# Moving, shortening and joining the branches around the rare token lots of a mixture of experts

## The chip, the cores and the metric

The kernel runs on one core of a Trainium2 chip, as one program. The metric is the device time of one execution in microseconds (us). The engines are named as the profile names them: PE (matrix products, with PEld for the weights that it loads), ACT, DVE, POOL, and SP, which issues the DMAs. A name with a q (PEq, SPq) is the engine's sequencer or its queue of DMAs.

## The reference, cut to what matters

The program is a first block of two dense layers and a second block of two layers. Each layer of the second block ends in a mixture of 32 experts in four groups: a router picks the best group of a token and two experts in it, and every token goes through its two experts. Layer 0 has 512 tokens (256 of `x` and 256 of the context), layer 1 has 256.

```python
def hier_moe(h, grp_w, grp_b, exp_w, exp_b, w_gate, w_up, w_down):
    g_logit = (h @ grp_w).astype(jnp.float32) + grp_b.astype(jnp.float32)
    g_idx = jnp.argmax(g_logit, axis=-1).astype(jnp.int32)
...
    top_v, top_i = lax.top_k(e_logit, TOP_K)
    w = (g_prob * jax.nn.softmax(top_v, axis=-1)).astype(h.dtype)
    e_idx = g_idx[:, None] * EXPERTS_PER_GROUP + top_i.astype(jnp.int32)
    return routed_experts(h, e_idx, w, w_gate, w_up, w_down)

    def expert_block(args):            # in routed_experts
        xblk, e = args
        return (jax.nn.silu(xblk @ w_gate[e]) * (xblk @ w_up[e])) @ w_down[e]
```

`w_gate` and `w_up` of an expert are 1024 x 512, `w_down` is 512 x 1024, all float32. How many tokens an expert gets is known only when the program runs.

## The kernel before, in words

Everything that the change touches is in `experts`, which writes the program of one layer's experts. It is written out without a loop over the experts: the 32 experts stand in the code one after the other, as 16 pairs, once for layer 0 and once for layer 1.

**Slots and lots.** An expert has CAP = 64 slots for tokens, in two lots of LOT = 32. The first lot is always computed. The second is computed inside `If(count > LOT)` (L2070), and whatever goes beyond 64 tokens inside `If(count > CAP)` (L2084, in `more`). Those are the rare lots. Their counts lie in the table `cnt`, and each of the engines that has work in the branch (PE, ACT, DVE, and POOL in layer 0) loads the count into a register (L1870) and jumps on its own. Entries from NE on hold the larger count of each pair; the kernel before uses only the last of these, the largest of all, after the experts (`rest`, L2142).

**A pair, in the order in which PE meets it.** The names S, M and J are this document's:

- `expert(p, 0)`: `gate_up` of the first lot (L2010, 64 products of 32 slots by 256 columns over four weight tiles), branch S0 (L2070), `combine` of half of the previous pair's result (L1986), `turn_lots` (two transposes, L1921), branch M0 (L2084), whose body `more_gate_up` gathers 32 more tokens and does `gate_up` for them.
- `expert(p, 1)`: the same for the second expert: `gate_up`, branch S1, the other half of `combine`, `turn_lots`, `slots` (transposes, L1945), branch M1.
- `down(p)`: `project` for both experts together (L1960, 32 products of 64 slots by 512 columns), which ACT and DVE then weigh (L1953, L1954), after every second pair `gather` for the next two pairs (L1895), and branches J0 and J1 (L2084 both), whose body `more_project` projects what `more_gate_up` left.

So PE meets six branches a pair, 96 a layer. Whether a body runs or not, its instructions stand in the program, and an engine that does not need them jumps over them.

**Weights.** A pair needs twelve tiles of 1 MB: four `gu` for each expert and four `down`. SP issues their DMAs (L315) in the order of use into rings of 1 MB buffers, 14 buffers in layer 0 and 18 in layer 1. A buffer is given to a later tile when the last instruction that could read it has been passed, which for `gu` is in the branches M0 and M1 and for `down` in J0 and J1. `K.addn` names the tiles of a step; a tile is given back after the last step that names it.

Of the kernel before, what the change touches and what calls it, by code (L numbers as in the profile page):

```python
# [11 lines left out]
F32R = mybir.dt.float32r  # L12
# [6 lines left out]
P = 128  # L19
# [1653 lines left out]
class _Moe:  # L1673
# [87 lines left out]
    def experts(self, i, rms=None, side=None, tail=None):  # L1761
# [150 lines left out]
        def lot(hs, i, xk, ws):  # L1912
            gu = K.pt("acc")[:, :256]
            gate_up(gu, xk, ws)
            hidden(hs[:, i * P:i * P + P], gu)

# [39 lines left out]
        def project(hTa, hTb, a0, b0, a1, b1, wsl):  # L1956
            ys = [K.pt("acc"), K.pt("acc")]
            for c, n in ((c, n) for b in (0, 2) for n in range(2) for c in (b, b + 1)):
                for s, (hT, ws) in enumerate(((hTa, (a0, a1)), (hTb, (b0, b1)))):
                    mm(ys[n][64 * s:64 * s + 64], lhsT=hT[:, at(c)], rhs=part(ws, c)[:, n * 512:n * 512 + 512],  # L1960
                       start=c == 0, stop=c == 3, tile_position=(0, 64 * s), skip_group_check=True)
            yh, yl = (B.new(n, [P, D], F32R) for n in ("yh", "yl"))
# [56 lines left out]
        def more_gate_up(Pm, wt, ws, parts):  # L2019
# [19 lines left out]
            turn(hs, hT)  # L2039

        def more_project(parts, ws):
            hT, PT, wsl = parts
            ps = K.pt("acc")[:, :256]
            for c, q in enumerate(quarters):
                by_quarter(ps, hT[:, q], lambda q: part(ws, c)[:, 256 * q:256 * q + 256], start=c == 0, stop=c == 3)
            yh, yl = more_new(F32R), more_new(F32R)
            weigh(yh, yl, ps, wsl)
            for d in range(KC):
                q = quarters[d // 2]
                f = slice(d % 2 * P, d % 2 * P + P)  # L2050
                ps = K.pt()[:, :N]
                kw = dict(rhs=PT[q], tile_position=(LOT * (d // 2), 0))
# [4 lines left out]
        def expert(p, s):  # L2057
            def fn(*ws):
                e = 2 * p + s
                if e == 0:  # L2060
# [3 lines left out]
                xg, hs = B._t[f"xg{p // 2}"], B._t[f"hs{s}"]  # L2064
                o = (p % 2) * 2 * CAP
                if s == 1:
                    pw = weighed(B._t[f"P{p // 2}"][:, :, o:o + 2 * CAP], B.wt[:, :, e - 1:e + 1])
                x = lambda i: lambda k: xg[:, k, o + s * CAP + i * LOT:o + s * CAP + i * LOT + LOT]
                lot(hs, 0, x(0), ws)
                with K.tc.If(count(e, engines[:3]) > LOT):  # L2070
                    lot(hs, 1, x(1), ws)
                if p > 0:
                    combine(s, *B.y)
                turn_lots(hs, B.new(f"hT{s}", [P, 4 * CAP]))
                if s == 1:
                    PT, wsl = B._t["slots"] = B.new("PT", [P, N], F32R), B.new("wsl", [P, 1], bufs=2)
                    slots(pw, PT, wsl)
                parts = B._t[f"more{s}"] = more_parts(s)
                more(e, lambda: more_gate_up(first_lot(e), wt(e), ws, parts))
# [6 lines left out]

        def down(p, turns):
            def fn(*ws):
                PT, wsl = B.slots
                if turns:  # L2090
                    pick((p + 1) // 2)()
                B._t["y"] = (*project(B.hT0, B.hT1, *ws, wsl), PT)
                if turns:
                    gather((p + 1) // 2)()
                for s in range(2):
# [173 lines left out]
```

## Time and profile before

| | us |
|---|---|
| median of 3 runs | 2289.48 (2288.54 to 4694.85) |
| the profiled execution | 2281.83 |
| its span, first to last instruction | 2280.1 |
| of that the experts of layer 0 | 996 to 1556 |
| of that the experts of layer 1 | 1783 to 2262 |

The two stages are read off the timeline: from the first gathered tokens to the last rare projection, and to the branch of `rest`. The profiled execution is a single one, and 7.65 us shorter than the median of the runs. In the rows below, a group of instructions shows its count, and in square brackets the idle time of the engine ahead of its first instruction and what ended it. "<-PEq L2084" means that PE's own sequencer, at a branch of line 2084, was the last thing before PE went on; "<-issue" that the engine waited for nothing that the profile shows.

### The profile page before, as it was taken

The numbers are of one execution on the slowest core, as the hardware profiler recorded it, in microseconds if no ns is written. First come the engines' busy times: TensorE is split into PE (matmuls) and PEld (weight loads), VectorE is DVE, ScalarE is ACT, GpSimd is POOL, SyncE is SP. The second block draws the span as 40 slices with busy tenths as digits, with TensorE's granted clock in tenths as the row PEclk, the third lists the DMA queues.
The fourth block names the chain that finished last, engine by engine and source line by source line (L and its number), as shares of the span: only waits on it lengthen the run. The fifth ranks groups of instructions, "written<-read, shape, count | busy, mean of one in ns | idle before, by whom it ended". The sixth has DMA issues, their size and how long they took to land. (4 is left out here: it accounts for less than half of the span.)

```text
span 2280.1 us, 40150 instructions
## 1 busy us (share of the span) xinstructions
PE 1937.3 (85%) x15978; PEld 1510.0 (66%) x15978; DVE 1059.4 (46%) x1974; ACT 750.7 (33%) x1347; POOL 450.4 (20%) x496
## 2 busy tenths in 40 slices
PE   7889999998799987888888978887999787777776
PEld 6768998987799866655555655554877444444443
DVE  7665774576567579533223432335554312122123
ACT  5554653553456355421111111113453111111111
POOL 4122420999954016100000000001000000000000
PEclk9899999999999999989999899998999889889898
DMA  6477566444355453669997799982224899999993
GB/s 238 175 300 268 213 240 243 165 137 159 111 177 175 168 186 138 239 273 369 380 382 318 303 388 377 380 322 70 95 74 193 335 406 414 413 386 418 408 411 137
DMA packets 86478, 603.51 MB, mean 265 GB/s; under 512 B 9632, under 2 KB 12064, under 8 KB 13856
## 3 DMA queue, kind: packets, MB, share of 16 engines
q1 hardware_dynamic: 86176, 599.24, 67.6%
q8 instruction: 219, 3.59, 0.6%
q14 instruction: 83, 0.68, 0.1%
HBM read 598.15 MB, written 1.05 MB: 263 GB/s over the span
## 5 line engine op out<-in xcount | busy, mean ns | idle before, releaser
L405 PE MATMUL mm<-xh,wh 128*128 128x256 f32 x1024 | 294.8, 288 | 20.4 <-ACT wh L382 16.3
L407 PE MATMUL mm<-xh,wl 128*128 128x256 f32 x1024 | 292.9, 286 | 9.5 <-DVE wl L383 8.5
L406 PE MATMUL mm<-xl,wh 128*128 128x256 f32 x1024 | 292.8, 286 | 0.6 <-DVE xl L480 0.3
L1960 PE MATMUL acc<-down,hT 128*64 128x512 f32 x1024 | 242.2, 619 | 37.6 <-PEq L2084 35.1
L2010 PE MATMUL acc<-gu,xg 128*32 128x256 f32 x2944 | 185.7, 411 | 47.6 <-PEq L2084 28.8
L405 PEld LDWEIGHTS mm<-xh,wh 128*128 128x128 f32 x1024 | 199.1, 194 | 30.9 <-ACT wh L382 17.4
L1910 DVE TENSOR_TENSOR hs<-hs,acc 128x128 f32<-128x128 f32 x81 | 23.3, 287 | 418.6 <-ACT hs L1909 404.6
L1960 PEld LDWEIGHTS acc<-down,hT 128*64 128x64 f32 x1024 | 131.2, 142 | 128.1 <-issue 101.5
L2010 PE MATMUL acc<-gu,xc 128*32 128x256 f32 x2240 | 156.8, 432 | 60.6 <-PEq L2084 49.4
L407 PEld LDWEIGHTS mm<-xh,wl 128*128 128x128 f32 x1024 | 198.7, 194 | 11.1 <-DVE wl L383 9.9
L406 PEld LDWEIGHTS mm<-xl,wh 128*128 128x128 f32 x1024 | 199.1, 194 | 1.8 <-DVE xl L480 1.6
L2010 PEld LDWEIGHTS acc<-gu,xg 128*32 128x32 f32 x2944 | 115.5, 118 | 115.7 <-issue 72.2
L2010 PEld LDWEIGHTS acc<-gu,xc 128*32 128x32 f32 x2240 | 91.1, 124 | 123.5 <-issue 62.5
L1909 ACT ACTIVATE hs<-acc 128x128 f32<-128x128 f32 x81 | 22.4, 277 | 410.1 <-PE acc L2010 404.4
L1954 DVE SCALAR_TENSOR_TENSOR yl<-acc,wsl,yh 128x512 fp32r<-128x512 f32 x64 | 48.0, 751 | 224.9 <-ACT yh L1953 209.6
L383 DVE TENSOR_TENSOR wl<-ffn_w_up,wh 128x1024 fp32r<-128x1024 f32 x96 | 130.3, 1382 | 28.6 <-ACT wh L382 28.6
L405 PE MATMUL mm<-hh,wh 128*128 128x256 f32 (+1 forms) x416 | 128.5, 309 | 7.6 <-DVE cv L1250 5.9
L882 DVE SCALAR_TENSOR_TENSOR hv<-mm,vec,hv 128x255 f32<-128x255 f32 x192 | 88.2, 480 | 85.1 <-ACT hv L877 81.1
L406 PE MATMUL mm<-hl,wh 128*128 128x256 f32 (+1 forms) x416 | 124.3, 299 | 0.7 <-DVE hl L480 0.4
L407 PE MATMUL mm<-hh,wl 128*128 128x256 f32 (+1 forms) x416 | 123.8, 298 | 0.5 <-DVE wl L383 0.3
L1953 ACT ACTIVATE yh<-acc,wsl 128x512 fp32r<-128x512 f32 x64 | 44.0, 687 | 239.5 <-PE acc L1960 239.5
L424 POOL TENSOR_TENSOR xc<-xc,tot 128x256 f32<-128x256 f32 x4 | 2.9, 728 | 596.7 <-ACT tot L421 596.7
(494 smaller groups left out, 4461.4 us busy)
## 6 DMA issues: line engine op xcount, KB each, us to landing
gu<-in_gu_dram SPq DMA_DIRECT2D x256, 1024.0 KB, 10.9
down<-in_down_dram SPq DMA_DIRECT2D x128, 1024.0 KB, 11.3
mod_w<-in_mod_w_dram SPq DMA_DIRECT2D x48, 1024.0 KB, 4.9
ffn_w_up<-in_ffn_w_up_dram SPq DMA_DIRECT2D x48, 1024.0 KB, 4.9
ffn_w_down<-in_ffn_w_down_dram SPq DMA_DIRECT2D x24, 1024.0 KB, 4.8
w_in_ab<-in_w_in_ab_dram SPq DMA_DIRECT2D x12, 1024.0 KB, 4.8
kv_w<-in_kv_w_dram SPq DMA_DIRECT2D x8, 1024.0 KB, 6.7
w_out_ab<-in_w_out_ab_dram SPq DMA_DIRECT2D x8, 1024.0 KB, 4.8
```

What stands on the lines that cost most here:

```text
L383: self.lows.append(lambda: nc.vector.tensor_sub(wl, src, wh))
L405: mm(out, lhsT=wh(k), rhs=xh(k), start=s, stop=False, **kw)
L406: mm(out, lhsT=wh(k), rhs=xl(k), start=False, stop=False, **kw)
L407: mm(out, lhsT=wl(k), rhs=xh(k), start=False, stop=e, **kw)
L424: eng.tensor_tensor(out, out, t, op=ALU.add)
L882: nc.vector.scalar_tensor_tensor(hv[:, s, d:], ps[:, s * T:(s + 1) * T - d], cw(2 - d, m), hv[:, s, d:], op0=ALU.mult, op1=ALU.add)
L1909: nc.scalar.activation(hs, gu[:, 0:P], AF.Silu)
L1910: nc.vector.tensor_mul(hs, hs, gu[:, P:2 * P])
L1953: nc.scalar.activation(yh, ps, AF.Identity, scale=wsl)
L1954: nc.vector.scalar_tensor_tensor(yl, ps, wsl, yh, op0=ALU.mult, op1=ALU.subtract)
L1960: mm(ys[n][64 * s:64 * s + 64], lhsT=hT[:, at(c)], rhs=part(ws, c)[:, n * 512:n * 512 + 512], start=c == 0, stop=c == 3, tile_position=(0, ...
L2010: mm(out[c], lhsT=lhsT, rhs=rhs(q), tile_position=(0, LOT * q), skip_group_check=True, **kw)
```

## The change

It has four parts, all in `experts`.

1. **M0 and M1 move.** M0 goes from behind `turn_lots` of the first expert to a place inside the second expert's `gate_up`, after its first tile (k = 0 and 1). M1 goes from behind `slots` to the middle of `project`, after the half b = 0.
2. **The code of the rare bodies gets shorter.** `more_gate_up` and `more_project` put two products side by side (`by_half`, 512 columns each, in two groups of 32 of PE's rows of output) in place of four (`by_quarter`, 256 columns).
3. **J0 and J1 are put in one branch** on the larger count of the pair (entry NE + p of `cnt`). The two inner branches stand inside it.
4. The steps are cut to fit: `expert` becomes `first`, `second_begins` and `second`, `down` becomes `down_begins` and `down`, and `project` runs half by half. The tiles of a step that reads them in a moved branch are named in that step too, so the first expert's `gu` tiles are given back after the moved M0, the second expert's after the moved M1. Within `project` the order of the products in a half (n, then c) is the one that stood there.

```diff
@@ gate_up, project
-        def gate_up(gu, xk, ws):
-            for k in range(KC):
+        def gate_up(gu, xk, ws, ks=range(KC)):
+            for k in ks:
...
+        def project(ys, b, hTs, a, b0, a1, b1):
+            ws = ((a, a1), (b0, b1))
+            for n, c in ((n, c) for n in range(2) for c in (b, b + 1)):
+                for s, hT in enumerate(hTs):
+                    mm(ys[n][64 * s:64 * s + 64], lhsT=hT[:, at(c)], rhs=part(ws[s], c)[:, n * 512:n * 512 + 512],
                        start=c == 0, stop=c == 3, tile_position=(0, 64 * s), skip_group_check=True)
@@ more_gate_up
-            gu = K.pt("acc")[:, :256]
-            at_block = lambda c: slice(c, c + LOT)
-            gate_up(gu, lambda k: xgm[:, at_block(k % 2 * P + k // 2 * LOT)], ws)
-            hs = more_new()[:, :P]
-            hidden(hs, gu)
+            gu = K.pt("acc")[:2 * LOT]
+            for k in range(KC):
+                w = ws[k // 2].rearrange("p (k h n) -> p k h n", k=2, h=2)[:, k % 2]
+                o = k % 2 * P + k // 2 * LOT
+                by_half(gu, xgm[:, o:o + LOT], lambda h: w[:, h], start=k == 0, stop=k == KC - 1)
...
+        def by_half(out, lhsT, rhs, **kw):
+            for h in range(2):
+                mm(out[quarters[h]], lhsT=lhsT, rhs=rhs(h), tile_position=(0, LOT * h), skip_group_check=True, **kw)
@@ more_project
-            for c, q in enumerate(quarters):
-                by_quarter(ps, hT[:, q], lambda q: part(ws, c)[:, 256 * q:256 * q + 256], start=c == 0, stop=c == 3)
+            for c in range(4):
+                o = c % 2 * 2 * LOT + c // 2 * LOT
+                by_half(ps, hT[:, o:o + LOT], lambda h: part(ws, c)[:, 512 * h:512 * h + 512], start=c == 0, stop=c == 3)
@@ the steps of a pair
+        def second_begins(p):
+            def fn(*ws):
+                gu = B._t["gu"] = K.pt("acc")[:, :256]
+                gate_up(gu, lots_of(p, 1)(0), ws[4:], range(2))
+                parts = B._t["more0"] = more_parts(0)
+                more(2 * p, lambda: more_gate_up(first_lot(2 * p), wt(2 * p), ws[:4], parts))
+            return fn
...
+        def down_begins(p, turns):
+            def fn(*ws):
+                e = 2 * p + 1
+                if turns:
+                    pick((p + 1) // 2)()
+                B._t["ys"] = [K.pt("acc"), K.pt("acc")]
+                project(B.ys, 0, (B.hT0, B.hT1), *ws[4:])
+                parts = B._t["more1"] = more_parts(1)
+                more(e, lambda: more_gate_up(first_lot(e), wt(e), ws[:4], parts))
+            return fn
 
         def down(p, turns):
...
-                for s in range(2):
-                    more(2 * p + s, lambda: more_project(B._t[f"more{s}"], ws[s::2]))
+                with K.tc.If(count(NE + p) > CAP):
+                    for s in range(2):
+                        more(2 * p + s, lambda: more_project(B._t[f"more{s}"], ws[s::2]))
@@ the order of the steps
         for p in range(NE // 2):
-            for s in range(2):
-                e = 2 * p + s
-                K.addn([(f"gu{l}", 4 * e + i) for i in range(4)], expert(p, s))
+            gus = [[(f"gu{l}", 4 * (2 * p + s) + i) for i in range(4)] for s in range(2)]
             turns = p % 2 and p < NE // 2 - 1
-            K.addn([(f"down{l}", 2 * (2 * p + s) + i) for i in range(2) for s in range(2)], down(p, turns))
+            gu0 = K.addn(gus[0], first(p))
+            gu1 = K.addn(gu0 + gus[1], second_begins(p))[4:]
+            K.addn(gu1, second(p))
+            downs = [(f"down{l}", 2 * (2 * p + s) + i) for i in range(2) for s in range(2)]
+            d = K.addn(gu1 + downs, down_begins(p, turns))[4:]
+            K.addn(d, down(p, turns))
```

What this does to PE's program is seen in the second pair (p = 1) of layer 0. A row is an instruction, with its line, its result and operands (the tiles and buffers by name) and a count of equal ones in a row; L1870 is the load of a count into a register, and the body of a branch stands between COMPARE_AND_BRANCH and UNCONDITIONAL_BRANCH.

Before, around the end of pair 0 on PE: the last of pair 0's project, then J0 and J1, then `gate_up` of the next expert. At the "..." stand sixteen more rows of the body of J0:

```order
L1870 TENSOR_LOAD cnt
L2084 COMPARE_AND_BRANCH
L2010 MATMUL acc<-down_10863,hTm_11144 32x256 x8
L2010 MATMUL acc<-down_11035,hTm_11144 32x256 x8
...
L2084 UNCONDITIONAL_BRANCH x2
L1870 TENSOR_LOAD cnt
L2084 COMPARE_AND_BRANCH
L2010 MATMUL acc<-down_10865,hTm_11353 32x256 x8
L2010 MATMUL acc<-down_11037,hTm_11353 32x256 x8
```

After, at the same place on PE:

```order
L1870 TENSOR_LOAD cnt
L2147 COMPARE_AND_BRANCH
L1870 TENSOR_LOAD cnt
L2125 COMPARE_AND_BRANCH
...
L2125 UNCONDITIONAL_BRANCH x2
L1870 TENSOR_LOAD cnt
L2125 COMPARE_AND_BRANCH
...
L2125 UNCONDITIONAL_BRANCH x2
L2147 UNCONDITIONAL_BRANCH
L2017 MATMUL acc<-gu_11000,xg 32x256 x8
```

One load and one jump now stand between a pair and the next where neither expert has more than 64 tokens, in place of two of each.

Before, at M0 of the second pair on PE: `turn_lots` (L1921), the branch, and `gate_up` of the second expert behind it.

```order
L1921 MATMUL mm<-cst,hs_10496 128x128 x2
L1870 TENSOR_LOAD cnt
L2084 COMPARE_AND_BRANCH
...
L2010 MATMUL acc<-gu_11039,rd 32x256 x8
L2010 MATMUL acc<-gu_11041,rd 32x256 x8
L2010 MATMUL acc<-gu_11233,rd 32x256 x8
L2010 MATMUL acc<-gu_11235,rd 32x256 x8
L1945 MATMUL mm<-cst,sq 128x128 x4
...
L2084 UNCONDITIONAL_BRANCH x2
L2010 MATMUL acc<-gu_11237,xg 32x256 x8
```

After, at the same place on PE:

```order
L1925 MATMUL mm<-cst,hs_10496 128x128 x2
L2017 MATMUL acc<-gu_11192,xg 32x256 x8
L1870 TENSOR_LOAD cnt
L2125 COMPARE_AND_BRANCH
...
L1949 MATMUL mm<-cst,sq 128x128 x4
...
L2125 UNCONDITIONAL_BRANCH x2
L2017 MATMUL acc<-gu_11194,xg 32x256 x8
```

The second expert's first eight products (one of its four tiles) now stand ahead of the branch, behind the transposes. M1 moves in the same way into `project`: before, all of L1960 stood behind it, after, the first half of them (now L1965) stands ahead of it.

## Rows read from the trace of the kernel before

**Rows 1.** Windows, the two stages: PE, PEld, DVE, ACT, POOL busy, PEclk, DMA share, GB/s

```profile
996.00:1556.00 560.00, 465.27 (x4468) 306.49 (x4459) 176.49 (x386) 81.98 (x188) 1.45 (x2) 0.94 0.86 346
1783.00:2262.00 479.00, 361.24 (x3284) 223.72 (x3272) 102.37 (x226) 69.44 (x160) 0.00 (x0) 0.90 0.95 385
```

**Rows 2.** Waits of PE, 996 to 1556: us in total, times, longest us

```profile
PE acc L2010 <- PEq L2084: 28.8, 19, 3.9
PE mm L1986 <- PEq L2070: 20.2, 15, 2.9
PE acc L2010 <- DMA gu<-in_gu_dram: 11.0, 6, 2.7
PE acc L1960 <- PEq L2084: 8.4, 12, 2.1
PE acc L2010 <- issue: 5.5, 4, 3.1
```

**Rows 3.** Waits of PE, 1783 to 2262

```profile
PE acc L2010 <- PEq L2084: 49.4, 31, 4.5
PE acc L1960 <- PEq L2084: 26.6, 15, 3.5
PE mm L1986 <- PEq L2070: 16.1, 25, 2.7
PE acc L2010 <- issue: 10.9, 8, 2.7
```

**Rows 4.** Timeline of PE, one pair's end, 1145 to 1157

```profile
1147.52 7.18 PE L1960 MATMUL acc<-down,hT 128*64 128x512 f32 x32 [0.55 <-PEq L2084]
1156.03 1.29 PE L2010 MATMUL acc<-gu,xg 128*32 128x256 f32 x20 [1.34 <-PEq L2084]
```

**Rows 5.** Timeline of PE in layer 1, 1985 to 2050

```profile
1995.96 0.36 PE L1986 MATMUL mm<-PT,yh 128*128 128x256 f32 x1 [0.30 <-PEq L2070]
2000.74 5.28 PE L2010 MATMUL acc<-gu,xc 128*32 128x256 f32 x64 [3.37 <-PEq L2084]
...
2012.48 9.73 PE L1960 MATMUL acc<-down,hT 128*64 128x512 f32 x32 [3.51 <-PEq L2084]
2027.30 3.66 PE L2010 MATMUL acc<-gu,xc 128*32 128x256 f32 x64 [1.12 <-PEq L2084]
```

**Rows 6.** Instructions at line 2084, 1783 to 2262: count, least/median/longest ns

```profile
L2084 PEldq COMPARE_BRANCH  x64: 208/346/5182, 1787.7 to 2260.6; - x64
```

**Rows 7.** The page's DMA queues: packets, MB, share of 16 engines

```profile
q8 instruction: 219, 3.59, 0.6%
```

**Rows 8.** Timeline of PE, 1096 to 1108: a wait with no branch ahead

```profile
1096.38 0.38 PE L1921 MATMUL mm<-cst,hs 128*128 128x128 f32 x2
1099.83 5.17 PE L2010 MATMUL acc<-gu,xg 128*32 128x256 f32 x64 [3.07 <-issue]
1107.14 0.47 PE L1986 MATMUL mm<-PT,yh 128*128 128x512 f32 x1 [2.14 <-PEq L2070]
```

**Rows 9.** Timeline of PE, 1228 to 1284: a rare lot's products

```profile
1242.45 3.66 PE L2010 MATMUL acc<-gu,rd 128*32 128x256 f32 x64 [0.47 <-ACT rd L1930]
...
1272.73 1.93 PE L2010 MATMUL acc<-down,hTm 128*32 128x256 f32 x32
```

**Rows 10.** Timeline of PE, 1531 to 1566: the other rare lot's products

```profile
1543.29 3.66 PE L2010 MATMUL acc<-gu,rd 128*32 128x256 f32 x64 [0.47 <-ACT rd L1930]
...
1556.02 1.93 PE L2010 MATMUL acc<-down,hTm 128*32 128x256 f32 x32 [0.82 <-ACTq L2084]
```

**Rows 11.** Waits of SP's DMA queue, 996 to 1556

```profile
SPq L315 <- PEq L2084: 411.8, 56, 32.0
```

**Rows 12.** Windows in layer 1, columns as in rows 1

```profile
1850.00:1900.00 50.00, 41.15 (x382) 26.64 (x374) 11.09 (x24) 7.76 (x19) 0.00 (x0) 0.93 1.00 406
2100.00:2150.00 50.00, 35.80 (x268) 22.89 (x270) 10.81 (x23) 8.07 (x18) 0.00 (x0) 0.86 1.01 415
...
2240.00:2245.00 5.00, 4.18 (x68) 2.94 (x69) 0.29 (x1) 0.28 (x1) 0.00 (x0) 1.00 0.07 26
```

**Rows 13.** Timeline of PE, 2244 to 2264: the last pair of layer 1

```profile
2252.85 7.20 PE L1960 MATMUL acc<-down,hT 128*64 128x512 f32 x32 [0.57 <-PEq L2084]
2262.06 0.35 PE L2109 MATMUL acc<-PT,yh 128*128 128x256 f32 x1 [2.01 <-PEq L2142]
```

**Rows 14.** DMAs issued, 1783 to 2262: count, KB, median us from issue to landing

```profile
gu<-in_gu_dram SPq DMA_DIRECT2D x114, 1024.0 KB, 12.0
down<-in_down_dram SPq DMA_DIRECT2D x60, 1024.0 KB, 12.1
```

More of the change, by code (lines that the diff above doesn't have):

```diff
@@ L1915, in lot, with second_lot @@
             hidden(hs[:, i * P:i * P + P], gu)
+        def second_lot(e, hs, xk, ws):
+            with K.tc.If(count(e, engines[:3]) > LOT):
+                lot(hs, 1, xk, ws)
         def turn_lots(hs, hT):
@@ L1954, in weigh, with weigh_pair @@
             nc.vector.scalar_tensor_tensor(yl, ps, wsl, yh, op0=ALU.mult, op1=ALU.subtract)
[L1956 to L1960, printed above, removed]
+        def project(ys, b, hTs, a, b0, a1, b1):
[3 more added lines that the diff above has]
+                    mm(ys[n][64 * s:64 * s + 64], lhsT=hT[:, at(c)], rhs=part(ws[s], c)[:, n * 512:n * 512 + 512],
                        start=c == 0, stop=c == 3, tile_position=(0, 64 * s), skip_group_check=True)
+        def weigh_pair(ys, wsl):
             yh, yl = (B.new(n, [P, D], F32R) for n in ("yh", "yl"))
@@ L2048, in more_project @@
+            yh, yl = (K.tile("sm", [P, 4 * P], F32R, "sq", 2)[:2 * LOT] for _ in range(2))
+            weigh(yh, yl, ps, wsl[:2 * LOT])
             for d in range(KC):
-                q = quarters[d // 2]
-                f = slice(d % 2 * P, d % 2 * P + P)
+                q = quarters[d // 4]
+                f = slice(d % 4 * P, d % 4 * P + P)
                 ps = K.pt()[:, :N]
-                kw = dict(rhs=PT[q], tile_position=(LOT * (d // 2), 0))
+                kw = dict(rhs=PT[q], tile_position=(LOT * (d // 4), 0))
@@ L2063, in fn, with second @@
                         nc.gpsimd.memset(B.new(n, [P, 2 * P]), 0.0)
-                xg, hs = B._t[f"xg{p // 2}"], B._t[f"hs{s}"]
-                o = (p % 2) * 2 * CAP
[L2066 to L2071, printed above, removed]
-                if p > 0:
[L2073 to L2079, printed above, removed]
+                x = lots_of(p, 0)
+                lot(B.hs0, 0, x(0), ws)
+                second_lot(e, B.hs0, x(1), ws)
+                if p > 0:
+                    combine(0, *B.y)
+                turn_lots(B.hs0, B.new("hT0", [P, 4 * CAP]))
+            return fn
[6 more added lines that the diff above has]
+            return fn
+        def second(p):
+            def fn(*ws):
+                e = 2 * p + 1
+                o = (p % 2) * 2 * CAP
+                x = lots_of(p, 1)
+                pw = weighed(B._t[f"P{p // 2}"][:, :, o:o + 2 * CAP], B.wt[:, :, e - 1:e + 1])
+                gate_up(B.gu, x(0), ws, range(2, KC))
+                hidden(B.hs1[:, :P], B.gu)
+                second_lot(e, B.hs1, x(1), ws)
+                if p > 0:
+                    combine(1, *B.y)
+                turn_lots(B.hs1, B.new("hT1", [P, 4 * CAP]))
+                PT, wsl = B._t["slots"] = B.new("PT", [P, N], F32R), B.new("wsl", [P, 1], bufs=2)
+                slots(pw, PT, wsl)
             return fn
@@ L2085, in more, with fn @@
                 fn()
+        def down_begins(p, turns):
+            def fn(*ws):
+                e = 2 * p + 1
+                if turns:
[4 more added lines that the diff above has]
+                more(e, lambda: more_gate_up(first_lot(e), wt(e), ws[:4], parts))
+            return fn
         def down(p, turns):
```

27 lines of the change are left out of this document (17 added, 10 removed).

## Prediction

> **What bounds the kernel now.** I began with the windows, to split the time by stage. The two stages that the change touches are 560 and 479 us long [rows 1]. In layer 0 PE is busy for 465 of 560 us and the DMA engines for 0.86 of the time; in layer 1 PE is busy for 361 of 479 us and the DMA engines for 0.95. So layer 0 hangs on PE, with some room in the DMAs, and layer 1 on both: PE waits a lot there, but the transfers have hardly any room.
>
> The waits of PE come next. In layer 0 five rows give 28.8 + 20.2 + 11.0 + 8.4 + 5.5 = 73.9 us [rows 2]; in layer 1 four rows give 49.4 + 26.6 + 16.1 + 10.9 = 103.0 us [rows 3]. Nearly all of it stands at branches. L1986 stands behind S0 and S1, L1960 behind M1, and L2010 behind M0 or behind J0 and J1. I count the row on `gu` tiles with them, since it names the same line, and a `gu` tile was in place by then.
>
> The timeline shows what a branch costs when nothing goes wrong, and when something does. Cheap ones: 0.30 us behind S [rows 5], 0.55 us behind M1, and 1.34 us behind J0 and J1 together [rows 4] (1.12 in layer 1 [rows 5]). Dear ones: 3.37 us behind M0 and 3.51 behind M1 [rows 5]. The branch instruction itself tells the same: at L2084 PE's takes 346 ns in the median and 5182 at the longest [rows 6]. The dear ones I put down to code that isn't there yet. Queue q8 carries PE's instructions in 219 packets with 3.59 MB [rows 7], 16.4 KB each; the built PE program of before has 56,869 instructions, so one takes 63 bytes, and a packet (a block, from here on) holds some 260. A jump over a body of 178 instructions (M0 in layer 0) often ends in a block that hasn't come. A wait of 3.07 us where no branch stands ahead at all [rows 8] fits that and no other reading that I have.
>
> Long waits have a second price. The granted clock is 0.94 and 0.90 in the two stages [rows 1]. [...]
>
> **The change part by part: layer 0.**
>
> *J0 and J1 become one branch.* A pair's two cost 1.34 and 1.12 us, say 1.2; a single cheap one costs 0.30 to 0.55. One goes: 16 x 0.7 = 11 us less. Bounds: 0 (the joined jump goes over 147 instructions instead of 103 and 103, and may miss its block), and 16 x 1.04 = 17.
>
> *M0 moves and its body shrinks.* L2010's waits are 28.8 + 11.0 + 5.5 = 45.3 us; less 16 x 1.2 at J that leaves 26 at M0. At a cheap price of 0.4 it would be 6, so 20 us are misses. The body goes from 178 to 116 instructions, so the share of jumps that leave a block falls by about a third (178/260 to 116/260), and 0.9 us of products (16 of 64 in 3.66) now stand between `turn_lots` and the jump, time for the next block. I take two thirds of the misses: 13 us less. Bounds: 0 (misses come elsewhere) and 20. The move alone doesn't take the cheap price away, as PE still ends its queue before it goes on.
>
> *S0 and S1* stay where they are, and their bodies stay as long. They wait 20.2 us, of which 32 x 0.3 = 10 is cheap. The whole program shrinks from 56,869 to 50,874 instructions, all of it here (5,995 in 32 pairs, 187 a pair), so fewer blocks are crossed: 5 less, bounds 0 and 10. *M1* waits 8.4 us, and its sixteen cheap prices are that alone: 1 less, 0 to 4.
>
> [...]
>
> *The rare bodies when they run.* Their products are half as many and twice as long in all, two side by side rather than four. They run for two experts, both in layer 0: `gate_up` there takes 3.66 us and the projection 1.93, twice [rows 9, 10]. The same columns with half the rows of PE at work: 2 x (3.66 + 1.93) = 11 us more. Bounds: 0 (were it the number of instructions that set the time) and 13. Nothing hides it, as PE is what is waited for.
>
> Sum for layer 0: -11 - 13 - 5 - 1 - 10 + 11 = -29 us, 560 to 531; ends +11 and -66, the latter only if all goes at once, which I don't believe past -45. SP's queue there waits 411.8 us for L2084 [rows 11], which means that the rings are full, not that loads come late. The later release (a first expert's `gu` by 0.9 us, a second's by half of `project`, 3.6 us) costs nothing as long as that holds.
>
> **Layer 1.** The same working on PE's side gives: J 16 x 0.7 = 11; M0 49.4 + 10.9 - 16 x 1.12 = 42, less 6 cheap, 36 of misses, two thirds 24; M1 26.6 - 16 x 0.57 = 17 of misses, a third 6; clock 15: together 56 us. But the transfers don't allow it. The stage moves 479 x 385 = 184 MB [rows 1], the last of it near 2243, 460 us in [rows 12]. The best stretches reach 415 GB/s at a share of 1.01 [rows 12], which would be 444 us: 16 us less at most. At the end, `project` of the last pair begins at 2252.85 [rows 13], 10 us behind the last landing; a PE that waits for tiles instead of branches would follow it closely, in some 3 us: 7 less. Sum: -23 us, bounds -4 (only the joined branch, and it hides) and -26. What is late next is the tile itself: waits of L2017 and L1965 for DMAs take the place of those for branches.
>
> `weigh_pair`, ACT and DVE run the same operations as before; M1 in the middle of `project` makes ACT and DVE jump there too, beside PE's products, at no cost: they are busy for 15 and 32% of layer 0 [rows 1]. If POOL or DVE came late at a branch it would be tenths of a us.
>
> **The sum.** -29 - 23 = -52; the blocks of all later code are also cut anew, which can move single misses by a few us either way; I round to -53. The working is made against the execution of 2281.83 us, which goes to 2229; the median of the runs is 7.65 above, so I forecast 2289.5 - 53 = 2236 us.
>
> [...]
>
> **The rivals.**
>
> *The waits stay.* The dear waits may hang on where a block begins rather than on how much is jumped, and then they move and don't shrink. Layer 0: J -11, bodies +11, nothing else: 0. Layer 1: J -11, of which the transfers pass on some. Time 2289.5 - 10 = 2280. For it: jumps S keep their length, and PE ends its queue at every branch wherever it stands. Against: bodies of 178 and 116 instructions can't miss blocks of 260 equally often. Chance 0.15.
>
> *Layer 1's gain is hidden by the transfers.* Layer 0 as above, layer 1 -4: 2289.5 - 33 = 2257. For it: shares of 1.00 and 1.01 in the middle of the stage. Against: PE's clock of 0.86 in the second of these windows, and the 10 us at the end. Chance 0.17.
>
> *All misses go.* [...] Chance 0.10.
>
> *Slower: the rings run dry.* `gu` of a second expert comes back 3.6 us later, and its four loads begin together that much later. A tile takes 10 to 12 us from issue to landing [rows 14]; with 18 buffers and 12 tiles a pair the reserve in layer 1 is some six tiles, 6 x 2.5 = 15 us, so 3.6 us are within it, but if the queue did idle for 3.6 us in each of the 16 pairs it would be 58 us; PE's savings there would not be seen, and the time would be 2289.5 - 29 + 58 = 2318. It decides from an idle time of 1.8 us a pair on. For it: the transfers are the bound of layer 1, so any idle time counts. Against: the queue waits for a buffer even now for most of the stage and still stays at 1.00. Chance 0.05.
>
> **How the numbers follow.** The forecast has 0.53. 2% (about what a measurement of this kernel can tell from no change) is 46 us, so faster begins below 2243.7. Of the forecast's cases, spread by some 15 us about 2236, I count 0.40 to faster and 0.13 to within 2%. With all misses gone that makes 0.50 and a little of the second rival (if layer 1 gives back half, 0.05): faster 0.55; within 2% 0.40; slower 0.05. The range goes from 2207 (beyond the third rival's) to 2277 (nearly to the first's); the forecast's own is 2218 to 2254.
>
> **What would show it.** Right: L1986's and L2017's waits at branches fall in sum to 45 us or less in layer 0, with one wait of about 0.5 us between pairs; q8 shows fewer packets (some 195); the clock is 0.96 or above in layer 0; the rare products take 7.3 and 3.9 us; the stage of layer 0 is some 30 us shorter; in layer 1 PE waits for DMAs of `gu` and `down`, the rate is near 415 GB/s throughout, and the stage is some 23 us shorter. Wrong: the dear waits are as many as before; or the DMA share in layer 1 falls below 0.95 while SP waits for L2125.

## The result and the profile after

The changed kernel takes 2220.4 us (median of 4 runs, 2217.29 to 2220.71) against 2289.0 us for the kernel before: a ratio of 0.970, 95% interval 0.968 to 0.972. It is faster by 68.6 us, or 3.0%. One of the four runs of the kernel before took 4694.85 us, and the ratio leaves it out. The forecast was 2236 us, 53 us faster, with a range of 2207 to 2277. The profiled execution of the changed kernel took 2220.28 us with a span of 2218.5 us, so the two profiles differ by 61.6 us; the other 7 us are those by which the profiled execution of before lay below its runs.

The windows of the changed kernel's two stages come first. The columns are as in [rows 1]; a stage runs from the first product of `gate_up` to the first product of `last`.

```profile
993.90:1529.70 535.80, 478.41 (x4450) 282.83 (x4448) 183.65 (x400) 84.81 (x192) 2.91 (x4) 0.96 0.89 361
1739.80:2201.00 461.20, 365.44 (x3313) 191.53 (x3313) 102.22 (x226) 70.06 (x161) 0.00 (x0) 0.96 0.97 401
```

Between the same two products the stages of before take 574.0 us (994.3 to 1568.3) and 480.9 us (1781.1 to 2262.1). So layer 0 gave 38.2 us, layer 1 gave 19.7 us, and what lies around them 4 us, though nothing was changed there; the two traces are single executions, so a few us of each difference are chance. PE's granted clock rose from 0.94 and 0.90 to 0.96 in both.

The waits of PE in layer 0 (us in total, times, longest us) answer to [rows 2]:

```profile
PE mm L1993 <- PEq L1918: 18.2, 14, 3.4
PE acc L2017 <- PEq L2125: 8.9, 15, 2.5
PE acc L2017 <- PEq L2147: 6.1, 13, 0.7
PE acc L2017 <- issue: 4.5, 4, 2.1
...
PE acc L1965 <- PEq L2125: 2.2, 14, 0.2
```

L1993 stands behind S0 and S1, L1965 behind M1, and L2017 behind M0 (L2125) or the joined J (L2147). Together they are 39.9 us, where [rows 2] had 73.9. M1 has become next to nothing: 14 waits of 0.16 us each. S is as large as it was. In layer 1 the waits answer to [rows 3]:

```profile
PE acc L2017 <- DMA gu<-in_gu_dram: 41.6, 35, 1.5
PE mm L1993 <- PEq L1918: 13.4, 22, 2.5
PE acc L2017 <- PEq L2125: 7.3, 11, 3.0
PE acc L2017 <- PEq L2147: 6.8, 15, 0.5
PE acc L1965 <- DMA down<-in_down_dram: 4.5, 5, 1.6
PE acc L2017 <- issue: 4.3, 3, 2.5
```

At branches and behind them PE waited for 103.0 us; now it waits for 32 us there and for 46 us for weights, and each wait of the latter kind ends within 0.2 us of a tile's landing. The transfers run without a gap in the middle of the stage, at 417 to 418 GB/s where [rows 12] had 406 to 415:

```profile
1800.00:1850.00 50.00, 43.79 (x461) 25.32 (x460) 13.37 (x30) 9.01 (x21) 0.00 (x0) 1.00 1.01 417
2050.00:2100.00 50.00, 40.87 (x398) 24.55 (x400) 11.67 (x27) 7.37 (x18) 0.00 (x0) 0.89 1.01 418
```

The timeline of PE around pair 5 of layer 0 shows each branch as it stands now, and answers to [rows 4, 5]:

```profile
1136.83 3.65 PE L1965 MATMUL acc<-down,hT 128*64 128x512 f32 x16
1140.64 3.66 PE L1965 MATMUL acc<-down,hT 128*64 128x512 f32 x16 [0.16 <-PEq L2125]
1144.75 3.66 PE L2017 MATMUL acc<-gu,xg 128*32 128x256 f32 x64 [0.45 <-PEq L2147]
1148.73 0.47 PE L1993 MATMUL mm<-PT,yh 128*128 128x512 f32 x1 [0.32 <-PEq L1918]
...
1150.98 1.07 PE L2017 MATMUL acc<-gu,xg 128*32 128x256 f32 x16
1153.89 2.37 PE L2017 MATMUL acc<-gu,xg 128*32 128x256 f32 x40 [1.84 <-PEq L2125]
```

From the top: half of `project`, M1 for 0.16 us, the other half, the joined J for 0.45, `gate_up`, S0 for 0.32, then the second expert's first 16 products and M0, which here waits 1.84 us. The cheap price is therefore not one number: 0.15 us, 0.18 (M0 at its cheapest), 0.32, 0.45, depending on what stands ahead. A tile's eight rows in the program order of "The change" are sixteen products in the trace, so M0 stands behind 16 products and M1 behind 16 of `project`.

Last, the rare products in layer 0, which answer to [rows 9, 10], and the queue of PE's instructions, which answers to [rows 7]:

```profile
1225.50 7.06 PE L2058 MATMUL acc<-gu,rd 128*32 128x512 f32 x32 [0.47 <-ACT rd L1934]
...
1255.14 3.63 PE L2058 MATMUL acc<-down,hTm 128*32 128x512 f32 x16
```

```profile
q8 instruction: 196, 3.21, 0.6%
```

7.06 - 3.66 + 3.63 - 1.93 = 5.1 us more for an expert, 10.2 for the two.

### The profile page after: what moved, and what is told of

It reads as the page before. It is cut to its first block, busy times and chain, and to the rows that moved or that the text cites. A ratio compares the mean times of both kernels' runs of the same rounds, so it can differ in the third digit from the quotient of the medians.

```text
span 2218.5 us, 39754 instructions
## 1 busy us (share of the span) xinstructions
PE 1938.9 (87%) x15884; PEld 1445.7 (65%) x15884; DVE 1060.0 (48%) x1974; ACT 751.1 (34%) x1347; POOL 450.4 (20%) x496
## 3 DMA queue, kind: packets, MB, share of 16 engines
HBM read 598.15 MB, written 1.05 MB: 270 GB/s over the span
## 5 line engine op out<-in xcount | busy, mean ns | idle before, releaser
L1965 PE MATMUL acc<-down,hT 128*64 128x512 f32 x1024 | 255.6, 607 | 10.3 <-DMA down<-in_down_dram 4.5
L2017 PE MATMUL acc<-gu,xc 128*32 128x256 f32 x2240 | 144.6, 394 | 61.3 <-DMA gu<-in_gu_dram 41.6
L2017 PE MATMUL acc<-gu,xg 128*32 128x256 f32 x2944 | 179.5, 394 | 20.5 <-PEq L2125 8.9
L1965 PEld LDWEIGHTS acc<-down,hT 128*64 128x64 f32 x1024 | 83.4, 139 | 159.8 <-issue 137.9
L2017 PEld LDWEIGHTS acc<-gu,xg 128*32 128x32 f32 x2944 | 111.6, 113 | 84.7 <-issue 36.3
L2017 PEld LDWEIGHTS acc<-gu,xc 128*32 128x32 f32 x2240 | 74.2, 112 | 127.2 <-DMA gu<-in_gu_dram 60.2
## 6 DMA issues: line engine op xcount, KB each, us to landing
gu<-in_gu_dram SPq DMA_DIRECT2D x256, 1024.0 KB, 18.3
```

The source lines that it names most:

```text
L2017: mm(out[c], lhsT=lhsT, rhs=rhs(q), tile_position=(0, LOT * q), skip_group_check=True, **kw)
```

## The experiments

Two theories were to be told apart. **A, queued work:** PE's sequencer runs ahead of PE. If enough products are queued ahead of a branch, the load of the count, the jump and the fetch of the code behind it all happen while PE still works, and only the end of the queue is seen. **B, code length:** a jump costs when it leaves the block of instructions at hand, so what counts is how long the bodies are. The kernel before ran beside each group of kernels; its median was 2282.7, 2280.0 and 2281.9 us in the three groups, so ratios are what is compared between groups, and otherwise the stages of the traces. Where a branch's waits are given as a sum (M0, S0 and so on), it is PE's idle time behind that branch where its body isn't run, added up over the pairs of a layer in the trace, whatever a view puts it down to; in the kernel before that gives, for layer 0, 23.0 us for S0 and S1, 27.4 for M0, 9.8 for M1 and 18.2 for J. The 30 and 12 us for M0 and M1 in the expectations hold 2.6 and 2.4 us more, the waits of PE for DVE in the two bodies that do run, which no branch causes. They have a row of their own among the waits of before in layer 0:

```profile
PE mm L2026 <- DVE sq L1875: 5.0, 2, 2.6
```

### e1_move: the moves alone

The edit is made in the changed kernel: both rare bodies are those of before, and J0 and J1 stand apart.

```diff
...
+            gate_up(gu, lambda k: xgm[:, at_block(k % 2 * P + k // 2 * LOT)], ws)
...
-                with K.tc.If(count(NE + p) > CAP):
-                    for s in range(2):
-                        more(2 * p + s, lambda: more_project(B._t[f"more{s}"], ws[s::2]))
+                for s in range(2):
+                    more(2 * p + s, lambda: more_project(B._t[f"more{s}"], ws[s::2]))
```

> The moved branches M0 and M1 alone: bodies as long as before, J0 and J1 apart. Theory A (queued work): the products ahead of the moved branch hide the load of the count, the jump and most of the fetch of code, so M0's waits in layer 0 fall from 30 us to about 10 and its cheap wait from 0.46-0.6 us to about 0.2 as in the changed kernel, though no code is shorter; layer 1 then follows the transfers: about 2289 - 45 = 2244 us, PE's instruction packets still 219 or so. Theory B (code length): the waits hang on how many blocks the jumps cross; with bodies as long as before hardly anything changes: 2280 us, M0 at 25 us or more in layer 0.

Measured: 2254.85 us, ratio 0.985 (0.980 to 0.990). Layer 0 takes 563.5 us, layer 1 462.6. q8 has 219 packets, as before. Both theories are half right. M1's waits are gone (0.15 to 0.16 us each in both layers), though its body is as long as ever. M0 keeps most of its misses: its waits add up to 18.6 us in layer 0 (27.4 before) and to 24.2 in layer 1 (30.1 before).

M1 in layer 1 shows theory A at its clearest. The first row is PE's branch instruction of M1 in one pair, with its duration in ns; the others are PE's timeline of e1_move around it:

```profile
L2113 PEldq COMPARE_BRANCH  x1: 3082/3082/3082, 1990.0 to 1990.0; - x1
```

```profile
1989.56 3.65 PE L1965 MATMUL acc<-down,hT 128*64 128x512 f32 x16
1993.37 3.19 PE L1965 MATMUL acc<-down,hT 128*64 128x512 f32 x13 [0.16 <-PEq L2113]
```

The branch takes 3.08 us, a miss like those of before, but it starts at 1990.0, while 16 products of `project` are queued until 1993.21, and PE stands still for 0.16 us. Nine of the sixteen M1 branches of that layer take over 1 us, and none is seen. At M0, with 0.9 us of products ahead, a miss of 2 to 3 us is seen for the most part. The first row is such a miss, the second a jump that was hidden:

```profile
1101.52 2.80 PE L2017 MATMUL acc<-gu,xg 128*32 128x256 f32 x48 [2.33 <-PEq L2113]
...
1141.40 6.25 PE L2017 MATMUL acc<-gu,xg 128*32 128x256 f32 x112 [0.18 <-PEq L2113]
```

### e2_join: J0 and J1 in one branch, alone

The edit is made in the kernel before.

```diff
-                for s in range(2):
-                    more(2 * p + s, lambda: more_project(B._t[f"more{s}"], ws[s::2]))
+                with K.tc.If(count(NE + p) > CAP):
+                    for s in range(2):
+                        more(2 * p + s, lambda: more_project(B._t[f"more{s}"], ws[s::2]))
```

> The kernel before with J0 and J1 in one branch, nothing else. Both theories: the wait between pairs falls from 1.12-1.34 us to 0.45 (the second load of a count and second jump, 0.3 + 0.34 us, came behind an empty queue), 16 x 0.75 = 12 us in layer 0 and about as much on PE in layer 1: 2289 - 20 = 2269 us, 2277 if layer 1 gives nothing. M0 and M1 wait as long as before (30 and 12 us in layer 0), give or take where blocks begin.

Measured: 2256.36 us, ratio 0.986 (0.981 to 0.990); layer 0 563.0 us, layer 1 476.4. That is 26 us less than the kernel before beside it, where 20 were expected at most; the traced execution, at 2261.17 us, is the slowest of the four, and its two stages show 15.5 of the 26. The waits in layer 0 (L2095 is the joined branch):

```profile
PE acc L2010 <- PEq L2084: 20.4, 9, 3.6
PE mm L1986 <- PEq L2070: 14.3, 16, 3.0
...
PE acc L2010 <- PEq L2095: 5.9, 13, 0.5
```

The join does what was said (13 waits, 5.9 us, where J took 18.2; the inner branches of the two pairs with a rare lot add 2.5). The rest isn't the join's: M0 and M1 together went from 37 to 43 us in layer 0, S from 23 to 17. So misses moved between branches here, some 6 us each way in layer 0. That they move because the later code comes to lie elsewhere in its blocks is a reading: no run shifts the code and does nothing else.

### e3_short: the shorter bodies alone

The kernel before, with the changed kernel's `more_gate_up` and `more_project`.

```diff
...
+                by_half(gu, xgm[:, o:o + LOT], lambda h: w[:, h], start=k == 0, stop=k == KC - 1)
...
```

> The kernel before with the shorter bodies, nothing else. Theory A: the rare products of two experts in layer 0 cost 11 us more; the waits at M0 fall by a few us at most: 2285 to 2298 us. Theory B: a third fewer of M0's and M1's jumps leave their block, in layer 0 30 + 12 us of waits become about 25, in layer 1 57 become 35; packets about 196: 2289 + 11 - 17 - 20 - 10 for the clock = 2253 us.

Measured: 2248.15 us, ratio 0.983 (0.979 to 0.987). That is 35 us less than the kernel before beside it: theory B's number (36 less), not A's (4 less to 9 more). Layer 0 takes 563.7 us although the rare products cost 10 us more there; layer 1 takes 460.1. In layer 0, M0's waits add up to 9.6 us where they were 27.4, with one miss above 1 us among the branches that aren't taken instead of eight; in layer 1 M0 goes from 30.1 to 12.8 and M1 from 27.0 to 16.2. q8 has 195 packets. So each of the two, moves and shorter code, brings layer 1 to 460 to 463 us alone, and the two together get it no further: in both kernels the DMA share over that stage is as in the changed kernel or above (0.97 and 0.98, at 400 and 401 GB/s), so most of it runs at the pace of the transfers.

### e4_move_join: everything but the shorter code

The changed kernel, with `more_gate_up` and `more_project` of before.

```diff
...
+            gate_up(gu, lambda k: xgm[:, at_block(k % 2 * P + k // 2 * LOT)], ws)
...
```

> The changed kernel with the long bodies of before (four groups of 256 columns): moves and the joined branch without the shorter code. Theory A: code length is worth little, and the 11 us that the short bodies cost on the two experts in layer 0 come back: 2220 - 8 = 2212 us (-11 +3). Theory B: long bodies bring the misses back: layer 0 +20, layer 1 hidden under the transfers or +5: 2220 + 20 + 5 - 11 = 2234 us.

Measured: 2231.07 us, ratio 0.975 (0.971 to 0.980); layer 0 540.2, layer 1 465.0. Theory A's number (2212, a ratio of 0.966) lies outside the interval, B's (2234) fits. From the changed kernel itself (0.970 and 0.973, measured twice) the time hardly tells it apart, since its rare products cost 10 us less. The misses are back at the two branches that have little queued ahead: S0 and S1 wait 28.5 us together in layer 0 (21.7 in the changed kernel), M0 13.8 (8.9). M1 is 2.4 us in both.

What the two theories each explain is seen best when PE's branches of these lines that take over 1 us are counted in the traces, over both layers. The five kernels with long bodies have 41 (before), 51 (e2_join), 53 (e1_move), 61 (e7_late) and 67 (e4_move_join); the seven traces of kernels with short bodies, with or without the moves and the join, have 28 to 33; e6_norare, without the rare bodies, has 4. So shorter code means fewer long jumps wherever the branches stand, and the moves make none of them short. Why the number goes from 41 to 67 among the long ones is open. That a long jump waits for code shows in the traces of before and of the changed kernel: each of the 41 in the one and of the 32 in the other ends 1.33 to 1.52 us after a packet of q8 has ended, a time that 15 of their 326 shorter jumps share. What stands ahead decides which are seen: in e1_move, e4_move_join and the changed kernel 36 of M1's jumps took over 1 us, and the longest gap behind one of them is 0.16 us.

### e5_move_short: everything but the join

```diff
-                with K.tc.If(count(NE + p) > CAP):
-                    for s in range(2):
-                        more(2 * p + s, lambda: more_project(B._t[f"more{s}"], ws[s::2]))
+                for s in range(2):
+                    more(2 * p + s, lambda: more_project(B._t[f"more{s}"], ws[s::2]))
```

> The changed kernel with J0 and J1 apart: the moves and the shorter bodies, not the join. The join saves the second load and jump, 16 x 0.75 = 12 us of PE in layer 0 and nothing in layer 1, where the transfers set the pace by now (460 us in the runs before): 2220 + 12 = 2232 us, layer 0 about 548 us, layer 1 about 461. If the join were worth as much as alone (26 us), 2246.

Measured: 2238.68 us, ratio 0.981 (0.978 to 0.984); layer 0 553.3 us, layer 1 461.7. By the ratios that is 18 to 24 us slower than the changed kernel, between the two numbers expected (12 and 26). Layer 0 is 17.5 us longer, layer 1 doesn't care, as expected. J's waits are 17.7 us in layer 0 again (6.5 and 2.3 for the inner branches in the changed kernel), which is 9 of the 17.5; S waits for 4 us more and M0 for 2 less, and the remaining 6 or so stay unexplained.

### e6_norare: no rare lots at all

```diff
         def more(e, fn):
-            with K.tc.If(count(e) > CAP):
-                fn()
+            return
...
-                with K.tc.If(count(NE + p) > CAP):
-                    for s in range(2):
-                        more(2 * p + s, lambda: more_project(B._t[f"more{s}"], ws[s::2]))
```

> Leaves out the rare lots: the branches M0, M1 and J with their bodies are not there, so the tokens beyond the 64th of two experts of layer 0 are missing. It bounds what these branches still cost. Layer 1: transfers set the pace, so 458 to 461 us as in the changed kernel; if it were still bound by PE's branches it would fall by their 21 us. Layer 0: the two rare lots themselves (some 2 x 16 us with gather, products and adding up), the waits at M0, M1 and J (9 + 2 + 7), and two thirds of the waits at S (code shorter still): 536 - 32 - 18 - 12 = 474, but the transfers of 192 tiles at 2.5 us allow 480 at least: about 485. Time about 2220 - 50 = 2170 us.

Measured: 2138.35 us, ratio 0.938 (0.935 to 0.941); layer 0 464.0 us, layer 1 450.9. Layer 0 fell by 72 us and is now bound by the transfers too. The first of these windows ends where the last tile lands, 5 us before the stage does:

```profile
994.00:1453.00 459.00, 422.59 (x4253) 247.32 (x4253) 161.41 (x355) 75.27 (x170) 0.00 (x0) 0.97 1.00 413
1666.00:2117.00 451.00, 366.99 (x3314) 186.13 (x3313) 100.36 (x228) 69.39 (x161) 0.00 (x0) 0.93 0.99 409
```

My expectation of 2170 us was 32 us too cautious, 21 of them in layer 0: its bound of 480 us counted all 192 tiles, of which 14 had landed before the stage began. It missed 10 us in layer 1: with 451 us at a share of 0.99 the transfers themselves weren't at their end with 461. Only the rare branches and their code are missing there, as no expert of layer 1 takes them. About half of the 10 us lie at the start of the stage. Its first 50 us, in the changed kernel and then in e6_norare:

```profile
1739.80:1789.80 50.00, 42.87 (x448) 24.09 (x448) 10.06 (x22) 10.78 (x23) 0.00 (x0) 1.00 0.89 357
1666.10:1716.10 50.00, 45.74 (x475) 25.64 (x478) 11.83 (x28) 11.23 (x24) 0.00 (x0) 0.97 0.97 394
```

That is 37 GB/s for 50 us, 1.85 MB, which I estimate as 4.4 us at 418 GB/s. In these 50 us of the changed kernel SP waits for PE at the branches M0 and M1, behind which `gu` buffers are given back:

```profile
SPq L315 <- PEq L2125: 18.4, 4, 7.9
```

So at the start of the stage the branches still set the pace of the transfers. Another 1.6 us lie between the last landing and the end of the stage (5.4 and 3.8 us); the rest stays open.

### e7_late: M0 behind more products

The edit is made in e4_move_join.

```diff
-                gate_up(gu, lots_of(p, 1)(0), ws[4:], range(2))
+                gate_up(gu, lots_of(p, 1)(0), ws[4:], range(6))
...
-                gate_up(B.gu, x(0), ws, range(2, KC))
+                gate_up(B.gu, x(0), ws, range(6, KC))
```

> As e4_move_join (long bodies), with M0 behind three tiles (48 products, 2.7 us) of the second expert's gate_up instead of one (16 products, 0.9 us). If all products ahead hide the fetch of code, M0's waits above 1 us go (13 in e4_move_join: 6 in layer 0, 7 in layer 1), as they did at M1 behind 3.6 us: M0 falls from 14 to 3 us in layer 0, 2231 - 14 = 2217 us. If PE's queue holds only so many products (at S, behind 64 of them, the load of the count began just 1.49 us before their end), the time won is 1.49 - 1.05 = 0.44 us a miss: M0 in layer 0 from 14 to 11 us, 2228 us.

Measured: 2245.15 us, ratio 0.984 (0.981 to 0.987): slower than e4_move_join, which neither reading foresaw. M0's own waits did fall, from 13.8 to 3.8 us in layer 0, though not by the queue alone, as three of its jumps there took over 1 us where eight had. But S1, which now follows M0 after 16 products instead of 48, went from 20.3 to 32.4 us. The waits and the timeline of layer 0:

```profile
PE mm L1993 <- PEq L1918: 35.9, 14, 5.0
...
PE acc L2017 <- PEq L2113: 3.5, 13, 0.7
```

```profile
1164.16 1.07 PE L2017 MATMUL acc<-gu,xg 128*32 128x256 f32 x16 [0.18 <-PEq L2113]
1169.42 0.77 PE L1993 MATMUL mm<-PT,yh 128*128 128x512 f32 x1 [4.19 <-PEq L1918]
```

In both kernels the same eight of S1's jumps in layer 0 take over 1 us. Together they take 34.3 us here and 27.4 in e4_move_join, 6.9 more, and the load of the count begins 1.0 us ahead of the queue's end, since only 16 products are left behind M0, where it mostly was 1.49; summed over the eight that is 5.3 us. The two make the 12.1 us. The second is the shorter queue. For the first I have a reading only: the time between the two jumps, in which the code could have come, is shorter. Queued work isn't the whole of it: at M0 the load of the count now begins 1.46 us before the queued products end (1.05 before), although 2.7 us of products stand ahead of it. So the sequencer is ahead by some 26 products (an estimate, 1.46 us at 57 ns each) and not by all 48. At S, behind 64 products of 3.66 us, the same shows: the load begins 1.49 us ahead of their end in the middle case. At M1 it is 3.63 us, all 16 products of `project`, which are twice as wide and four times as long (228 ns each instead of 57).

### e8_split, e9_after, e9_split, e10_split3: part of combine ahead of S

If work queued ahead is what hides a branch, S is the place left, and `combine` behind it has wide products (512 columns in layer 0). The edit is made in the changed kernel, for each of the two experts; part 0 is the first four of the eight products, part 1 the other four.

```diff
...
+                if p > 0:
+                    combine(0, *B.y, part=0)
                 second_lot(e, B.hs0, x(1), ws)
                 if p > 0:
-                    combine(0, *B.y)
+                    combine(0, *B.y, part=1)
```

> The changed kernel with half of combine (4 of 8 products, in layer 0 512 columns wide) ahead of S0 and S1, half behind. The queue ahead of S then holds 0.9 us of combine more: the load of the count should begin some 2.2 us before the queue ends instead of 1.49, the cheap wait at S goes from 0.32 to 0.16 us, a miss costs 0.7 us less: S0 + S1 in layer 0 from 22 to about 14 us, layer 1 the same 461 us: 2220 - 7 = 2213 us. Where the second lot runs (14 times in layer 0), only half of combine covers its hidden step: 14 x 0.2 = 3 us back. If waits at S hang on where blocks begin alone: 2220 +- 4.

Measured: 2212.86 us, ratio 0.970 (0.968 to 0.973); layer 0 528.6 us, layer 1 461.7. The ratio is that of the changed kernel as first measured, on another chip, so the two ran once more side by side, with a third.

> The changed kernel once more, beside e9_split and e10_split3 on one chip, since the kernel before came out between 2280 and 2289 us from chip to chip. Ratio to the kernel before 0.970 as first measured; whatever e8_split is worth over it must show within this call.

> e8_split again (half of combine ahead of S0 and S1): layer 0 was 529 us against 536 for the changed kernel, layer 1 the same, so 7 us less than e9_after (0.3%), if the traces tell the truth; if the two chips differed, no difference within 2 us.

> Three of combine's four parts ahead of S0 and S1 in layer 0 (1.4 us of wide products), one behind; layer 1 as in e9_split. If the queue ahead is what counts, the load of the count begins near 2.6 us before its end, S0 + S1 in layer 0 fall from 13 to 10 us: 3 us less than e9_split. Where the second lot does run (14 times in layer 0) only 0.5 us is left to cover its hidden step of 0.6 us and more: 14 x 0.5 = 7 us back, and then it is 4 us slower than e9_split.

Measured on one chip: the changed kernel 2221.38 us (2218.25 to 2226.71), ratio 0.973 (0.970 to 0.976); e9_split 2211.43 (2207.27 to 2213.23), ratio 0.968 (0.965 to 0.971); e10_split3 2212.39 (2208.01 to 2216.93), ratio 0.969 (0.966 to 0.972). So half of `combine` ahead of S gains 10 us over the change, and the six runs of the one lie wholly below those of the other; a third quarter of it changes nothing. The waits of layer 0, first of e9_after, then of e9_split (one line lower in the code, so L1994 is `combine`):

```profile
PE mm L1993 <- PEq L1918: 18.4, 15, 3.3
```

```profile
PE mm L1994 <- PEq L1918: 8.9, 11, 1.9
```

S0 and S1 together go from 21.3 to 11.9 us, layer 0 from 534.9 to 527.5, layer 1 stays at 461.8 and 461.7. The load of the count now begins 2.3 us ahead of the end of the queue (1.5 before), and the cheap wait at S0 falls from 0.36 to 0.15 us. In e10_split3 the lead is 2.8 and S falls to 10.1 us, as expected; the 7 us back that I expected where the second lot runs don't show in the time, which is 1 us above e9_split's with runs that overlap. `turn_lots` now waits right behind S, in place of `combine`:

```profile
PE mm L1925 <- DVEq L1918: 8.9, 13, 0.7
```

## Why the prediction came out as it did

**Right in direction, place and range.** Layer 0 hung on PE and its branches, layer 1 came to hang on the transfers, and both stages moved that way: -38.2 and -19.7 us against -29 and -23. The sum of -52 was short by 10 us between the profiles: 9 in layer 0 and 4 outside the two stages, less 3 that layer 1 gave below the forecast. That the total lies 15.6 us below the forecast is thus for the most part layer 0's. Its terms, each beside what the traces show:

- *J*, forecast -11: 18.2 us became 6.5 and 2.3 for the inner branches, so -9. In e2_join the joined branch is 0.45 us a pair as worked out.
- *M0*, forecast -13, measured -18.5 (27.4 to 8.9).
- *M1*, forecast -1, measured -7.4 (9.8 to 2.4). Two of its waits were misses of 1.9 and 2.1 us, which the forecast left out.
- *S*, forecast -5, measured -1.3 (23.0 to 21.7). The working counted 32 cheap prices, but 14 of the 32 bodies run, so more of the 23 us were misses than it took.
- *The rare bodies*, forecast +11, measured +10.2.
- *Not in the forecast*: PE's first waits for DVE in the two bodies that run went from 5.0 to 1.6 us, -3.4; products now stand ahead of them.
- *The clock*, forecast -10: no run changes the clock alone, so none shows this term, nor the 15 us in the sum for PE in layer 1 or the 10 us in the expectation of e3_short. The traces' records of the granted clock have two values, 0.50 and 1.00. All 19 stretches at 0.50 in layer 1 of the kernel before begin during a wait of PE of 1.9 us or more, or at most 2.2 us behind its end. Behind the wait of 3.37 us in [rows 5] the clock is 0.50 for 3.41 us, and `gate_up` takes 5.28 us instead of 3.66: 1.62 us more, half of that time. In layer 0 the time at 0.50 went from 72.8 to 37.9 us, with PE busy for 62.9 and 36.5 of it (in layer 1 from 95.6 to 41.0, busy for 76.2 and 38.7). At a half that is -13, an estimate. The other terms make -30 and this -43, 5 beyond the stage's -38.2, so the terms are not exact to a few us.

**The step that failed** is the sentence "The move alone doesn't take the cheap price away, as PE still ends its queue before it goes on". PE does still end its queue, and that costs 0.15 to 0.18 us. What I took for its price, 0.4 to 0.55 us, was for the most part the load of the count and the jump (some 0.3 us each) that began too late to be covered: in layer 0 of the kernel before, the load began 0.54 us (M0) and 0.61 us (M1) ahead of the end of PE's queue, in the middle case, and in the changed kernel 1.05 and 3.63 us. e1_move shows it with no code shortened: M1 costs 0.16 us, even where its jump takes 3.08 us. From the same error comes the working that M1's "sixteen cheap prices are that alone". The load's duration in the changed kernel (least, middle and longest ns) stands beside that of the jump in [rows 6]; M0 and M1 used to stand behind a few short transposes, with little else queued:

```profile
L1870 PEldq TENSOR_LOAD <-cnt x164: 295/302/488, 996.5 to 2195.7; - x164
```

**Layer 1 came out near its forecast partly by luck.** The -23 was 16 us from a better rate and 7 from the end of the stage. By the traces, the time from the start of the stage to the last landing went from 462.0 to 455.8 us, -6, and from there to the end of the stage from 19.0 to 5.4 us, -14. The rate of 415 GB/s "throughout" was the step that failed: the middle reached 418, but the first 50 us had 367 before and 357 after.

**Two workings that don't hold.** The wait of 3.07 us in [rows 8] is not one without a branch: M0 stands right ahead of it, and its jump was a short one, done some 3 us before the products began:

```profile
L2084 PEldq COMPARE_BRANCH  x1: 219/219/219, 1096.6 to 1096.6; - x1
```

There is a wait with no branch near it in layer 1 of the kernel before, where the last jump began 4.9 us before and products ran in between, and this row, not the one in [rows 8], shows that waits come in straight code too:

```profile
1974.00 1.51 PE L2010 MATMUL acc<-gu,xc 128*32 128x256 f32 x12 [2.69 <-issue]
```

In both rows the products begin as far behind a packet of q8 as the long jumps end: 1.35 us in this one, 1.43 us in [rows 8].

And the ends of layer 0's sum, +11 and -66, don't follow from the bounds of its terms, which give +13 and, with 18 us for the clock, -69; neither the forecast nor the range hangs on them.

**The step that held** is that shorter code means fewer misses. e3_short and e4_move_join show it from both sides, and the count of long jumps in all kernels agrees. I gave S a share of that gain (-5); it got next to none in this layer, since S had no more queued ahead than before, and misses move between branches. That M0 now lies closer to S1 may have a part in it; e7_late supports this, but it was not isolated.

**The rivals.** That the waits stay is refuted by e1_move and e3_short. That layer 1's gain is hidden by the transfers is half true: of the 56 us that the forecast gave PE there, 20 were seen. The rings did not run dry: the share is 1.01 in the middle of layer 1, and its first 50 us have 0.89 where before had 0.90. Loads took 20 us from issue to landing, as this view of the DMAs issued in layer 1 of the changed kernel shows beside [rows 14], which fits loads that are issued earlier than before and queue behind each other:

```profile
gu<-in_gu_dram SPq DMA_DIRECT2D x114, 1024.0 KB, 20.0
down<-in_down_dram SPq DMA_DIRECT2D x60, 1024.0 KB, 19.9
```

**The parts don't add up.** Alone, the moves, the join and the shorter code are worth 28, 26 and 35 us (2282.7 less each), 89 in all; together they gave 60 to 69. The loss is in layer 1, where they gave 18.3, 4.5 and 20.8 us alone but only 19.7 together, because most of that stage runs at the transfers' rate. In layer 0 it is the reverse: 10.5, 11.0 and 10.3 alone, 38.2 together. Why it is that much more than their sum there was not taken apart.

## What to carry to other kernels

In these kernels a branch that is almost never taken cost what wasn't hidden of the load of its count (0.3 us), its jump (0.35 us in the median and 5.18 at the longest [rows 6]) and the fetch of the code behind it. So put it in the middle of a run of long products, where the sequencer was furthest ahead here (3.63 us at M1), and not right behind short ones (0.54 to 0.61 us in the kernel before) or another jump. The body counts although it never runs: kernels with long bodies had 41 to 67 jumps of over 1 us, those with short ones 28 to 33. Sum such savings by stage, and stop at the rate of the transfers (418 GB/s in layer 1): each of two parts alone took in layer 1 what the whole change took.

## What was not expected of the hardware

- How far PE's sequencer was ahead depended on the length of the products queued, not on how many stand in the code: 1.49 us behind 64 products of 256 columns, 3.63 us behind 16 products of 512 columns.
- A branch of 3.08 us left a gap of 0.16 us, so a long jump and the working off of the queue go on side by side.
- Two jumps with 16 short products between them (e7_late) cost more than with 48: S1 in layer 0 went from 20.3 to 32.4 us, its longest wait to 5.0. Of the 12.1 us, 5.3 are the shorter queue ahead of S1 and 6.9 jumps that took longer.
- Moving a branch behind queued work did not make its jump shorter: the jumps of over 1 us are 41 to 67 in the kernels with long bodies and 28 to 33 in those with short ones, wherever the branches stand.
